# A two-layer mixer trunk on one core: the order of layer B's projection blocks, the pace of its convolutions, and the way its chunk-end decays are spread

## The chip, the cores and the metric

The kernel runs on one NeuronCore of one Trainium2 chip. The metric is the device time of one execution in microseconds (us). Before the change three runs gave 1652.05, 1648.64 and 1646.65 us; the median is 1648.64 us.

## The reference

A trunk of two layers over an input of 1024 tokens by 1024 features, float32. Each layer normalises, mixes, and adds to the stream; layer A is a chunked spatial gating unit, layer B a Mamba-2 state-space mixer. The change lies in the front part of layer B, which reads, cut down:

```python
proj = h @ w_in                                   # 1024 x 1024 by 1024 x 6176
z, xbc, dt_raw = proj[:2048], proj[2048:6144], proj[6144:]     # columns
xbc = silu(causal_depthwise_conv(xbc, conv_w, conv_b))         # 4 taps along the tokens
x, Bm, Cm = split(xbc)                                         # 8 groups of 256, 128, 128 columns
dt = softplus(dt_raw + dt_bias)                                # 32 heads
dA_cs = cumsum(dt * A, within each chunk of 128 tokens)
chunk_decay = exp(dA_cs[:, :, -1])                             # 8 chunks x 32 heads
# ... states, carried from chunk to chunk with chunk_decay; y; y * silu(z); norm; @ w_out
```

## The kernel before, in words

Matmuls are in float32 by three products of split operands: each operand is a high part (a cast, written on ACT, L111) and a low part (the rest, written on DVE, L112), and `mm3` (L134 to L136) issues high x high, low x high, high x low. A 128x512 output tile over 512 rows of depth is thus 12 matmuls; that is called a unit here.

Layer B's projection of z (four blocks `zb[0]` to `zb[3]`; `zb[3]` is narrow, 128 columns wide where the others have 256) and of half the groups of x, B and C (four blocks, `x` and `bc` for two pairs of groups) runs as blocks of Strassen's kind: seven products each, in the order 1, 2, 6, 7, 5, 4, 3, of two units each, or of one unit in the narrow block. ACT copies products 1, 6 and 7 to SBUF (`u`, L292); products 2, 5, 4 and 3 complete the quadrants C11, C22, C21 and C12. `into_b` runs `zb[0]` and the first product of `zb[1]`; `blocks` (L1400) runs the rest, in the order of its list `bs`. The weights of a block are loaded during the block before it (SP loads `wr`; POOL issues accumulating loads for sums and differences).

What is done with a quadrant:

- In a z block, an add on DVE (L960, except for C21, which is read from the accumulator), then SiLU on ACT (L965) and a store to DRAM, `z_d`, that ACT's queue issues (L966). SiLU and store are put off: a function goes into the list `late`.
- In an x or bc block, an add on DVE into `u` (L1304), a copy of three columns (`halo`, L1308), and one or two entries in the list `todo`: each is a convolution of a 128x512 tile. A convolution is an identity with scale and bias on ACT (L1271, into `xc`), three taps on DVE (L1265, and with a halo three small ones, L1268), SiLU on ACT (L1296) and a store from ACT's queue (L1297). SiLU and store go into `late`. A block leaves eight convolutions.

The order of the instructions is written out by hand here (`manual_schedule`): each engine has its instructions in the order in which the Python code issues them, and runs them strictly in that order. Ahead of each unit, `between` (L1412) runs the put-off work of `late`, and on odd turns, once the decays are through, also starts a convolution. Behind the last block convolutions are issued until three are left (`LEFT`), then the first split of plain weights (`next(pj)`) and a new set of PSUM pools, `new_psum` (L1455); the first matmuls of the plain projection write `ab`, in PSUM that the blocks' accumulators `acc` had. The rest of the convolutions is started by `scans`. During the last block, whose successor is none, three pieces of preparation for that projection are issued: the loads of its first weights at product 6, a load of 1 MB (`f01`) at product 7, and its split (`hh` and `hl`, 128x2048) at product 4.

`decays` (L1195) is a generator; `next(small)` advances it by one step at each unit, from the first unit of `blocks` on. It turns the raw `dt` into `dt`, `cs` (the cumulative sums) and `dtw` (`ecs` = exp(cs), `dte`), 32 heads by 128 tokens in four blocks of partitions. It stores `cs` and `ecs` to DRAM (L1234, eight stores of 32 KB, issued on SP's queue, two in each of four steps), and in the same steps the last column of each chunk of `ecs` to `dec_d` (L1237, eight stores of 32 single values each). Then PE transposes `dt`, `dte` and `cs` into PSUM tiles `tp` (L1246, two rotating buffers), one step each, and ACT copies each to `tk` (L1248) in the step behind. Last, SP loads `dec_d` broadcast over the partitions into `tk` (L1249).

Every DMA that SP's or ACT's queue issues signals one of eight completion counters, taken in turn; an issuing instruction waits until the DMA that used that counter before has landed.

Of the kernel before, what the change touches and what calls it, by code (L numbers as in the profile page):

```python
# [8 lines left out]
F32 = mybir.dt.float32  # L9
# [6 lines left out]
P = 128  # L16
# [7 lines left out]
NH = 32  # L24
# [5 lines left out]
def kernel(  # L30
# [21 lines left out]
    nc = tc.nc  # L52
    x = x[0]
    out = out[0]
# [8 lines left out]
    dr = ctx.enter_context(tc.tile_pool(name="dr", bufs=1, space=DRAM))  # L63

    def s8(shape, name, dt=F32):
        return sb.tile(shape, dt, name=name, tag="s8", bufs=16)

    def q4(shape, name):
        return sb.tile(shape, F32, name=name, tag="q4", bufs=6)

    def k2(shape, name, dt=F32):
        return sb.tile(shape, dt, name=name, tag="k2", bufs=4)
# [4 lines left out]
    def tiny(shape, name):  # L77
        return sb.tile(shape, F32, name=name, tag="tiny", bufs=8)
# [18 lines left out]
    def sm(name):  # L97
        return ps[0].tile([P, 512], F32, name=name, tag="sm", bufs=n_sm[0])
# [440 lines left out]
    tp = sm("tp")  # L539
# [12 lines left out]
    for gp in range(G // 2):  # L552
# [4 lines left out]
        if gp == 1:  # L557
# [9 lines left out]
            for h in range(2):  # L567
                tp = sm("tp")
# [5 lines left out]
                tp = sm("tp")  # L574
# [370 lines left out]
    late = []  # L945

    def finish():

        while late:
            late.pop(0)()  # L950
# [59 lines left out]
    zb = [z_block(b) for b in range(4)]  # L1010
# [184 lines left out]
    def decays():  # L1195

        dtw = q4([P, 4, 256], "dtw")
        cs = q4([P, 256], "cs")
        e_, s_, s2, p_ = (dtw[:, i, :] for i in range(4))
        V.scalar_tensor_tensor(e_, dtr, -1.0, dtr, ALU.mult, ALU.min)  # L1200
        nc.scalar.activation(e_, e_, AF.Exp)
        yield
        V.tensor_scalar(s_, e_, 2.0, None, ALU.add)
        V.reciprocal(s_, s_)
        V.tensor_tensor(s_, s_, e_, ALU.mult)
        V.tensor_tensor(s2, s_, s_, ALU.mult)
        V.tensor_scalar(p_, s2, 1.0 / 17, None, ALU.mult)
        for k in range(7, 0, -1):
            if k == 4:
                yield  # L1210
            V.scalar_tensor_tensor(p_, p_, 1.0 / (2 * k + 1), s2, ALU.add, ALU.mult)
        yield
        V.scalar_tensor_tensor(p_, p_, 1.0, s_, ALU.add, ALU.mult)
        V.tensor_scalar(s2, dtr, 0.0, None, ALU.max)
        dt = dtr
        V.scalar_tensor_tensor(dt, p_, 2.0, s2, ALU.mult, ALU.add)
        dA = dtw[:, 0, :]
        V.tensor_scalar(dA, dt, nA, None, ALU.mult)
        for j in range(2):
            V.tensor_tensor_scan(cs[:, j * P:(j + 1) * P], ones, dA[:, j * P:(j + 1) * P], 0.0, ALU.mult, ALU.add)  # L1220
        yield
        ecs = dtw[:, 1, :]
        nc.scalar.activation(ecs, cs, AF.Exp)
        dte = dtw[:, 2, :]
        for j in range(2):
            V.tensor_scalar(dte[:, j * P:(j + 1) * P], cs[:, j * P:(j + 1) * P], cs[:, j * P + P - 1:j * P + P], -1.0,
                            ALU.subtract, ALU.mult)
        yield
        nc.scalar.activation(dte, dte, AF.Exp)
        dec_d = dr.tile([8, NH], F32, name="dec_d")  # L1230
        for q in range(4):
            rs_ = slice(q * 32, (q + 1) * 32)
            for sc, src in ((cs_d, cs), (ecs_d, ecs)):
                nc.sync.dma_start(out=sc[2 * q:2 * q + 2].rearrange("c h l -> h c l"),  # L1234
                                  in_=src[rs_, :].rearrange("h (c l) -> h c l", c=2))
            for j in range(2):
                nc.sync.dma_start(out=dec_d[2 * q + j].rearrange("(h o) -> h o", o=1),  # L1237
                                  in_=ecs[rs_, j * P + P - 1:j * P + P])
            yield
        tk = s8([P, 2048], "tk")  # L1240
        tok = tk[:, 0:768].rearrange("p (v c r) -> p v c r", v=3, c=2)
        decb = tk[:, 768:1024]
        for i, src in enumerate((dt, dte, cs)):
            tp = sm("tp")
            for j in range(2):
                nc.tensor.transpose(out=tp[:, j * P:(j + 1) * P], in_=src[:, j * P:(j + 1) * P], identity=ident)  # L1246
            yield
            nc.scalar.copy(out=tok[:, i], in_=tp[:, 0:256].rearrange("p (c r) -> p c r", c=2))  # L1248
        nc.sync.dma_start(out=decb, in_=dec_d.rearrange("c h -> (c h)").partition_broadcast(P))  # L1249
        tok_of.update(tok=tok, decb=decb)  # L1250

    xbc_d, todo = {}, []

    def convolve():

        finish()
        if todo:
            late.append(todo.pop(0)())
# [15 lines left out]
    def xbc_block(kind, gs):  # L1274

        held, halos = {}, {}

        def cols(j):
            if kind == "x":
                return [(DI + gs[j] * 256, 256)]  # L1280
            return [(2 * DI + j * 1024 + g * P, P) for g in gs]

        def W(kh, j):
            return [b_w_in[kh * 512:(kh + 1) * 512, c:c + n] for c, n in cols(j)]

        def out(th, i, j, src, halo=None):
            if kind == "x":
                g, m, c = gs[j], i, cols(j)[0][0] + i * P
            else:
                g, m, c = gs[i], 2 + j, cols(j)[i][0]  # L1290
            dst = k2([P, 512], "xc")
            for op in conv_ops(dst, src, (c - DI) // P, halo):
                op()

            def rest():
                nc.scalar.activation(dst, dst, AF.Silu)  # L1296
                nc.scalar.dma_start(out=xbc_d[g][:, th, m, :], in_=dst)  # L1297

            return rest

        def done(name, i, a, u):
            th, j = 2 - int(name[1]), int(name[2]) - 1
            if u is not None:
                nc.vector.tensor_tensor(out=u, in0=a, in1=u, op=ALU.add)  # L1304
                a = u
            if th == 0:
                halo = halos[i, j] = tiny([P, 8], "halo")[:, 0:3]
                nc.vector.tensor_copy(out=halo, in_=a[:, 509:512])  # L1308
                todo.append(lambda: out(0, i, j, a))
                if (i, j) in held:  # L1310
                    todo.append(lambda: out(1, i, j, held[i, j], halo))
            elif (i, j) in halos:
                todo.append(lambda: out(1, i, j, a, halos[i, j]))
            else:
                held[i, j] = a

        return Block(H2, W, False, done, None)

    def rest_a21():
        raw = s8([P, 4, 512], "f01")  # L1320
        nc.sync.dma_start(out=raw, in_=f01_d)
        yield
        H2.update(new_H(("A21",)))
        split(*H2["A21"], raw)
# [75 lines left out]
    def blocks():  # L1400


        ORDER = (1, 2, 6, 7, 5, 4, 3)
        for g in SPILT:
            xbc_d[g] = dr.tile([P, 2, 4, 512], F32, name=f"xbc_d{g}")
        pairs = SPILT[:2], SPILT[2:]
        bs = [zb[1], xbc_block("x", pairs[0]), zb[2], xbc_block("bc", pairs[0]), zb[3], xbc_block("x", pairs[1]),
              xbc_block("bc", pairs[1])]
        seq = [(k, n) for k in range(len(bs)) for n in ORDER]
        small, turn, a21 = decays(), [0], rest_a21()  # L1410

        def between():  # L1412
            turn[0] += 1
            if next(small, 0) == 0 and turn[0] % 2:
                convolve()
            else:
                finish()

        for at, (k, n) in enumerate(seq[1:], 1):
            b, nxt = bs[k], bs[k + 1] if k + 1 < len(bs) else None  # L1420
            if at + 1 < len(seq):
                k2_, n2 = seq[at + 1]
                if n2 not in bs[k2_].Y:
                    bs[k2_].prep(n2)
            if n == 2:
                b.fourth()
            if nxt is not None:
                if n == 1 or at == 1:
                    nxt.load(0, 1)
                if n == 6:  # L1430
                    nxt.load(0, 0)
                elif n == 7:
                    nxt.sums_a()
                elif n == 5:
                    nxt.load(1, 0)
                    nxt.sums_b()
                elif n == 4:
                    nxt.load(1, 1)
            elif n == 6:
                next(pj)  # L1440
            elif n == 7:
                next(a21)
            elif n == 4:
                next(a21, None)
            for i in range(b.units):
                between()
                b.mm(n, i)
        while len(todo) > LEFT:
            convolve()

# [473 lines left out]
```

## Time and profile before

| what | value |
|---|---|
| median of three runs | 1648.64 us |
| the profiled execution: device time | 1643.76 us |
| the profiled execution: span of the trace | 1642.0 us |
| granted TensorE clock, mean | 0.965 |
| PE busy | 1511.4 us (92% of the span) |
| DVE busy | 1056.3 us (64%) |
| ACT busy | 775.9 us (47%) |
| POOL busy | 459.1 us (28%) |

The profile is one execution, recorded instruction by instruction. PE is the matmul engine, DVE VectorE, ACT ScalarE, POOL GpSimd, SP SyncE; `ACTq` and `SPq` are instructions with which ACT or SP issue DMAs. `L136` is line 136 of the kernel; `out<-in` names the tiles. An entry in square brackets is the idle time of the engine just before the instruction, and what ended it. The layer-B blocks discussed here take the time from about 793 to 1064 us of the span.

### The profile page before, as it was taken

What the parts mean: (1) busy time and instruction counts of PE and PEld (TensorE: products, weight loads), DVE (VectorE), ACT (ScalarE), POOL (GpSimd) and SP (SyncE); (2) the same over time, 40 slices, a digit from 0 to 9 for tenths busy, and PEclk for the clock granted to TensorE, in tenths of its full rate; (3) what the DMA queues carried; (4) which work ended last, traced back from release to release, by engine and by line L of the source; (5) the groups of instructions that cost most, each with busy time, mean ns of one, the idle gap of its engine ahead of it and who ended that gap; (6) DMA issues with size and microseconds to landing.
All of it is one profiled execution on the core that took longest, in us unless ns stands there. A gap on an engine that the chain in (4) does not pass through costs nothing.

```text
span 1642.0 us, 21287 instructions
## 1 busy us (share of the span) xinstructions
PE 1511.4 (92%) x7832; PEld 1242.2 (76%) x7832; DVE 1056.3 (64%) x1684; ACT 775.9 (47%) x1245; POOL 459.1 (28%) x466
## 2 busy tenths in 40 slices
PE   5799999999999999888979999969999999969988
PEld 5799988888888788766867777757777767747766
DVE  6966566666666545678525456756766767658746
ACT  4523233333333345545644455546666576543544
POOL 3601100000000141244301222116776756321231
PEclk7999999999999999988989999979999999979989
DMA  5154323333336999821577779745666675795992
GB/s 169 51 181 141 105 82 108 107 108 107 108 108 219 288 245 232 185 84 52 124 135 157 157 147 193 207 139 154 167 175 180 169 192 122 236 233 174 234 236 106
DMA packets 187784, 259.31 MB, mean 158 GB/s; under 512 B 16688, under 2 KB 117920, under 8 KB 184480
## 3 DMA queue, kind: packets, MB, share of 16 engines
q1 hardware_dynamic: 134672, 166.43, 33.9%
q0 software_dynamic: 39808, 70.53, 22.1%
q10 hardware_dynamic: 13200, 20.98, 3.6%
q8 instruction: 62, 1.02, 0.3%
q14 instruction: 42, 0.34, 0.1%
HBM read 183.65 MB, written 51.18 MB: 143 GB/s over the span
## 4 chain that ended last, share of the span: by engine, by line
PE 63%; DMA 12%; DVE 9%; ACT 8%; issue 5%; POOL 1%; ACTq 1%; SPq 1%; POOLq 0%; DVEq 0%
PE acc L136 12%; PE acc L134 11%; PE acc L135 11%; DMA wl<-cs_d 4%; PE ab L134 3%; PE ab L136 3%; PE ab L135 3%; PE ao L135 2%; PE ao L136 2%; PE ao L134 2%; PE yy L1557 2%; DVE xc L1265 2%; PE yy L1561 2%; PE mx L635 2%; DMA z_d<-zt 2%
## 5 line engine op out<-in xcount | busy, mean ns | idle before, releaser
L134 PE MATMUL acc<-hh,wh 128*128 128x512 f32 x868 | 344.3, 397 | 10.5 <-ACT wh L111 6.3
L136 PE MATMUL acc<-hh,wl 128*128 128x512 f32 x868 | 342.3, 394 | 6.0 <-DVE wl L112 6.0
L135 PE MATMUL acc<-hl,wh 128*128 128x512 f32 x868 | 340.8, 393 | 0.0
L112 DVE TENSOR_TENSOR wl<-wr,wh 128x1024 fp32r<-128x1024 f32 (+1 forms) x99 | 121.0, 1223 | 149.3 <-ACT wh L111 149.3
L134 PEld LDWEIGHTS acc<-hh,wh 128*128 128x128 f32 x868 | 165.1, 190 | 49.1 <-ACT wh L111 8.8
L136 PEld LDWEIGHTS acc<-hh,wl 128*128 128x128 f32 x868 | 164.8, 190 | 45.2 <-DVE wl L112 10.8
L135 PEld LDWEIGHTS acc<-hl,wh 128*128 128x128 f32 x868 | 164.8, 190 | 33.6
L111 ACT CAST wh<-wr 128x1024 fp32r<-128x1024 f32 (+1 forms) x113 | 116.4, 1030 | 109.3 <-PE acc L135 58.8
L292 ACT COPY u<-acc 128x512 f32<-128x512 f32 x117 | 67.9, 585 | 195.9 <-PE acc L136 191.4
L136 PE MATMUL acc<-wh,hl 128*128 128x256 f32 x448 | 130.4, 291 | 13.3 <-DVE hl L395 13.3
L134 PE MATMUL acc<-wh,hh 128*128 128x256 f32 x448 | 131.2, 293 | 4.1 <-DVE vt L331 2.5
L134 PE MATMUL ab<-hh,wh 128*128 128x512 f32 x256 | 116.8, 456 | 17.9 <-DVE xc L1265 17.9
L135 PE MATMUL acc<-wl,hh 128*128 128x256 f32 x448 | 129.7, 290 | 1.3 <-DVE wl L405 1.3
L1531 ACT ACTIVATE wl<-wl,tk 128x128 f32<-128x128 f32 x256 | 82.2, 392 | 80.3 <-DMA wl<-cs_d 80.0
L136 PE MATMUL ab<-hh,wl 128*128 128x512 f32 x256 | 101.7, 397 | 0.0
L135 PE MATMUL ab<-hl,wh 128*128 128x512 f32 x256 | 101.2, 395 | 0.0
L136 PEld LDWEIGHTS acc<-wh,hl 128*128 128x128 f32 x448 | 88.9, 199 | 14.4 <-DVE hl L395 14.4
L134 PE MATMUL bo<-wh,xh 128*128 128x512 f32 x192 | 80.5, 419 | 17.7 <-ACT xh L111 11.4
L112 DVE TENSOR_TENSOR xl<-ya,xh 128x1024 fp32r<-128x1024 f32 x40 | 49.0, 1224 | 68.7 <-ACT xh L111 68.7
L134 PEld LDWEIGHTS acc<-wh,hh 128*128 128x128 f32 x448 | 89.0, 199 | 5.2 <-issue 2.9
L135 PEld LDWEIGHTS acc<-wl,hh 128*128 128x128 f32 x448 | 89.0, 199 | 1.7 <-DVE wl L405 1.5
L111 ACT CAST xh<-ya 128x1024 fp32r<-128x1024 f32 x40 | 42.1, 1053 | 96.8 <-PE ao L135 43.1
(321 smaller groups left out, 3328.9 us busy)
## 6 DMA issues: line engine op xcount, KB each, us to landing
wr<-in_a_w_in_dram SPq DMA_DIRECT2D x48, 512.0 KB, 5.0
wl<-cs_d SPq DMA_DIRECT2D x64, 256.0 KB, 7.3
wr<-in_b_w_in_dram SPq DMA_DIRECT2D x30, 512.0 KB, 3.9
ya<-ya POOLq DMA_DIRECT2D x28, 512.0 KB, 15.1
wb<-in_a_w_out_dram SPq DMA_DIRECT2D x10, 1024.0 KB, 7.8
wb<-in_b_w_out_dram SPq DMA_DIRECT2D x10, 1024.0 KB, 13.5
wr<-in_b_w_in_dram SPq DMA_DIRECT2D x36, 256.0 KB, 8.2
v<-v_d SPq DMA_DIRECT2D x8, 1024.0 KB, 5.0
```

Source lines behind the costliest of these rows:

```text
L111: nc.scalar.copy(out=hi, in_=src)
L112: return (eng or nc.vector).tensor_tensor(out=lo, in0=src, in1=hi.bitcast(F32), op=ALU.subtract)
L134: nc.tensor.matmul(out=o, lhsT=l[0], rhs=r[0], start=start, stop=False, **kw)
L135: nc.tensor.matmul(out=o, lhsT=l[0], rhs=r[1], start=False, stop=False, **kw)
L136: nc.tensor.matmul(out=o, lhsT=l[1], rhs=r[0], start=False, stop=stop, **kw)
L292: nc.scalar.copy(out=self.u[n][:, i], in_=a)
L635: nc.tensor.matmul(out=mx[:, q * P:(q + 1) * P], lhsT=v[:, th * 4 + q, m * P:(m + 1) * P], rhs=mw[:, 0, :], start=True, stop=True)
L1265: nc.vector.scalar_tensor_tensor(dst[:, s:], src[:, :n - s], convw(3 - s, ch), dst[:, s:], ALU.mult, ALU.add)
L1531: nc.scalar.activation(wl[:, j, :], wl[:, j, :], AF.Relu, scale=-1.0, bias=tokc(2, c, self.g)[:, j:j + 1])
L1557: nc.tensor.matmul(out=yy[f * 64:(f + 1) * 64, pt * P:(pt + 1) * P], lhsT=w[:, j * 64:(j + 1) * 64], rhs=wl[:, j, :], start=True, stop=True)
L1561: nc.tensor.matmul(out=yy[:, 256 + pt * P:384 + pt * P], lhsT=self.state[c - 1][:, pt * P:(pt + 1) * P], rhs=self.x(3, c), start=True, sto ...
```

## The change

Four things, all inside `decays` and `blocks`:

1. In the list `bs` the narrow block `zb[3]` goes from the fifth place to the last; the second pair's x and bc blocks each move up by one.
2. `between` is replaced by `unit`. It sets the put-off work aside, starts a convolution if the decays are through and either the turn is odd or more than three are waiting, issues the unit's matmuls with the copies or adds behind them, and only then the put-off work.
3. `dec_d`, its eight stores and its broadcast load go. Instead ACT copies the last column of each chunk of `ecs`, broadcast to 128 columns, into the free quarter of `dtw` (`last`, two copies), PE transposes `last` like the three others, and ACT copies the result to `decb`.
4. `decays` has one step more behind the exponential of `dte`, and one more for the fourth transpose.

```diff
@@ decays
         nc.scalar.activation(dte, dte, AF.Exp)
-        dec_d = dr.tile([8, NH], F32, name="dec_d")
+        yield
         for q in range(4):
...
-            for j in range(2):
-                nc.sync.dma_start(out=dec_d[2 * q + j].rearrange("(h o) -> h o", o=1),
-                                  in_=ecs[rs_, j * P + P - 1:j * P + P])
             yield
...
-        for i, src in enumerate((dt, dte, cs)):
+        last = dtw[:, 3, :]
+        for j in range(2):
+            nc.scalar.copy(out=last[:, j * P:(j + 1) * P],
+                           in_=ecs[:, j * P + P - 1:j * P + P].broadcast_to([P, P]))
+        for i, src in enumerate((dt, dte, cs, last)):
...
-            nc.scalar.copy(out=tok[:, i], in_=tp[:, 0:256].rearrange("p (c r) -> p c r", c=2))
-        nc.sync.dma_start(out=decb, in_=dec_d.rearrange("c h -> (c h)").partition_broadcast(P))
+            if i < 3:
+                nc.scalar.copy(out=tok[:, i], in_=tp[:, 0:256].rearrange("p (c r) -> p c r", c=2))
+            else:
+                nc.scalar.copy(out=decb.rearrange("p (q j h) -> p j q h", q=4, j=2),
+                               in_=tp[:, 0:256].rearrange("p (j q h) -> p j q h", j=2, q=4))
@@ blocks
-        bs = [zb[1], xbc_block("x", pairs[0]), zb[2], xbc_block("bc", pairs[0]), zb[3], xbc_block("x", pairs[1]),
-              xbc_block("bc", pairs[1])]
+        bs = [zb[1], xbc_block("x", pairs[0]), zb[2], xbc_block("bc", pairs[0]), xbc_block("x", pairs[1]),
+              xbc_block("bc", pairs[1]), zb[3]]
...
-        def between():
+        def unit(b, n, i):
             turn[0] += 1
-            if next(small, 0) == 0 and turn[0] % 2:
-                convolve()
-            else:
-                finish()
+            off = late[:]
+            late.clear()
+            if next(small, 0) == 0 and todo and (turn[0] % 2 or len(todo) > 3):
+                late.append(todo.pop(0)())
+            b.mm(n, i)
+            for f in off:
+                f()
...
             for i in range(b.units):
-                between()
-                b.mm(n, i)
+                unit(b, n, i)
```

On SP, where the decays are stored (`cs`, `ecs` in `dtw`; `wr` is a load of weights), the kernel before has:

```order
L1234 DMA cs_d<-cs 32x2x128
L1234 DMA ecs_d<-dtw 32x2x128
L1237 DMA dec_d<-dtw 32x1 x2
L120 DMA wr<-in_b_w_in_dram 128x4x256
L1234 DMA cs_d<-cs 32x2x128
L1234 DMA ecs_d<-dtw 32x2x128
L1237 DMA dec_d<-dtw 32x1 x2
```

and the changed one, from the same place on:

```order
L1234 DMA cs_d<-cs 32x2x128
L1234 DMA ecs_d<-dtw 32x2x128
L1234 DMA cs_d<-cs 32x2x128
L1234 DMA ecs_d<-dtw 32x2x128
L120 DMA wr<-in_b_w_in_dram 128x4x256
L1234 DMA cs_d<-cs 32x2x128
L1234 DMA ecs_d<-dtw 32x2x128
```

The single-value stores are gone from between the pairs, and one load of weights that stood behind the first pairs now stands ahead of them.

On ACT, at the end of the blocks (the cast `wh` is for the plain projection, `xc` are convolutions, `zt` the z tiles, `acc` the blocks' accumulators), the kernel before has:

```order
L111 CAST wh_8214<-wr_8138 128x1024
L1296 ACTIVATE xc_8091<-xc_8091 128x512
L1297 DMA xbc_d5_6216<-xc_8091 128x512
L1271 ACTIVATE xc_8111<-acc_7820,par_867 128x512
L1296 ACTIVATE xc_8111<-xc_8111 128x512
L1297 DMA xbc_d3_6215<-xc_8111 128x512
L1271 ACTIVATE xc_8118<-u_7834,par_867 128x512
L1296 ACTIVATE xc_8118<-xc_8118 128x512
L1297 DMA xbc_d3_6215<-xc_8118 128x512
L1271 ACTIVATE xc_8128<-acc_7821,par_867 128x512
```

and the changed one, up to the first convolution of the plain projection (`x_8237<-ab_8188`):

```order
L111 CAST wh_8238<-wr_8162 128x1024
L966 DMA z_d6_5296<-zt_8106 128x512
L1275 ACTIVATE xc_8133<-u_7781,par_867 128x512
L965 ACTIVATE zt_8128<-acc_7980 128x512
L1300 ACTIVATE xc_8133<-xc_8133 128x512
L966 DMA z_d6_5296<-zt_8128 128x512
L1301 DMA xbc_d5_6216<-xc_8133 128x512
L965 ACTIVATE zt_8153<-zt_8153 128x512
L966 DMA z_d6_5296<-zt_8153 128x512
L1275 ACTIVATE x_8237<-ab_8188,par_867 128x1024
```

Before, convolutions follow each other there, two of them reading accumulators (`acc_7820`, `acc_7821`); now one convolution stands there, which reads `u`, and the SiLUs of the narrow block's last tiles, one of which reads an accumulator (`acc_7980`).

On ACT, during product 6 of `zb[2]` (`t12` is a weight sum to be cast for a later product), the kernel before has:

```order
L1271 ACTIVATE xc_6857<-acc_6507,par_867 128x512
L292 COPY u_6874<-acc_6769 128x512
L1296 ACTIVATE xc_6857<-xc_6857 128x512
L1297 DMA xbc_d0_6213<-xc_6857 128x512
L292 COPY u_6874<-acc_6770 128x512
L111 CAST wh_6891<-t12_6606 128x1024
```

and the changed one:

```order
L1275 ACTIVATE xc_6868<-u_6583,par_867 128x512
L292 COPY u_6888<-acc_6773 128x512
L965 ACTIVATE zt_6855<-zt_6855 128x512
L966 DMA z_d4_5294<-zt_6855 128x512
L292 COPY u_6888<-acc_6774 128x512
L1300 ACTIVATE xc_6868<-xc_6868 128x512
L1301 DMA xbc_d1_6214<-xc_6868 128x512
L111 CAST wh_6907<-t12_6602 128x1024
```

The convolution's SiLU and store stood ahead of the unit's second copy and now stand behind it; the cast stands behind both, as before.

## The prediction

> **What bounds the kernel now.** I read the page first (PE is busy 92% of the span), then, for the stretch that the change touches, PE's waits between 780 and 1120 us:
>
> ```profile
> PE ab L134 <- DVE xc L1265: 17.9, 1, 17.9
> PE tp L1246 <- ACT tk L1248: 8.2, 1, 8.2
> PE acc L134 <- ACT wh L111: 4.3, 4, 1.8
> PE acc L136 <- DVE wl L112: 2.8, 7, 0.5
> PE acc L134 <- ACT u L292: 2.7, 5, 0.8
> PE acc L134 <- ACT xc L1296: 1.4, 1, 1.4
> ```
>
> The columns are the total, the number of waits and the longest. PE bounds the stretch; two waits, 26.1 us together, stand out, and the blocks' other waits sum to 11.2 us. So the question is what these two hang on. The windows (us, then busy PE, PEld, DVE, ACT, POOL, granted clock, DMA share, GB/s) show each as a hole in PE, and the blocks between as nearly full:
>
> ```profile
> 823.60:831.80 8.20, 0.02 (x1) 0.00 (x0) 0.28 (x1) 1.95 (x4) 0.00 (x0) 0.64 1.44 159
> 832.00:1063.90 231.90, 221.01 (x938) 176.80 (x937) 132.24 (x206) 122.65 (x166) 46.32 (x36) 0.98 0.77 164
> 1063.90:1081.70 17.80, 0.03 (x1) 0.00 (x0) 11.77 (x16) 5.38 (x8) 2.75 (x1) 0.62 0.29 100
> ```
>
> In the first hole nobody computes and the DMA share is high: a transfer is waited for. In the second DVE is busy for 11.8 of 17.8 us: work is waited for.
>
> The first hole, on ACT's timeline and on the chain of waits:
>
> ```profile
> 830.08 0.33 ACTq L966 DMA_DIRECT2D z_d<-zt  x1
> 830.44 1.04 ACT L111 CAST wh<-wr 128x1024 fp32r<-128x1024 f32 x1 [6.21 <-DMA z_d<-zt]
> 831.39 0.37 ACT L1248 COPY tk<-tp 128x256 f32<-128x256 f32 x1
> ```
>
> ```profile
> 814.06 15.94 DMA z_d<-zt
> ```
>
> ACT's queue stands at the issue of a `z_d` store until 830.08, since an earlier `z_d` store with the same completion counter, issued at 814.06, lands only after 15.94 us. Behind it in ACT's order stand a cast and the copy of the transpose; PE's third transpose needs that copy for its buffer. So PE waits for a slow store. Three kinds of transfer between 806 and 841 us (size, median time to landing), then `z_d` between 885 and 930 us:
>
> ```profile
> cs_d<-cs SPq DMA_DIRECT2D x4, 32.0 KB, 9.6
> ecs_d<-dtw SPq DMA_DIRECT2D x4, 32.0 KB, 7.0
> dec_d<-dtw SPq DMA_DIRECT2D x8, 0.1 KB, 15.0
> ```
>
> ```profile
> z_d<-zt ACTq DMA_DIRECT2D x8, 256.0 KB, 2.9
> ```
>
> The same store lands in 2.9 us later on and takes 15.94 us here. The slowest beside it, by far the slowest for their size, are the `dec_d` stores: 128 bytes in 15.0 us. On SP they hold the queue, too:
>
> ```profile
> 823.04 5.19 SPq L1237 DMA_DIRECT2D dec_d<-dtw  x2
> ```
>
> **Part by part: the decays.** The change takes away the eight `dec_d` stores, and their broadcast load. With them the reason that I see for the slow landing goes, the `z_d` store is back near 2.9 us, and ACT does not stand. PE's rows there:
>
> ```profile
> 831.81 0.69 PE L1246 MATMUL tp<-ident,cs 128*128 128x128 f32 x2 [8.19 <-ACT tk L1248]
> 832.15 0.78 PE L134 MATMUL acc<-hh,wh 128*128 128x512 f32 x1
> ...
> 835.71 0.56 PE L136 MATMUL acc<-hh,wl 128*128 128x512 f32 x1
> ```
>
> ```profile
> 1063.32 0.39 PE L135 MATMUL acc<-hl,wh 128*128 128x512 f32 x1
> 1063.55 0.39 PE L136 MATMUL acc<-hh,wl 128*128 128x512 f32 x1
> 1081.78 0.77 PE L134 MATMUL ab<-hh,wh 128*128 128x512 f32 x1 [17.85 <-DVE xc L1265]
> ```
>
> Removed are 8.19 us of waiting, and the slow matmuls behind it: from 832.15 to 835.71 eight matmuls take 3.56 us, at the usual 0.23 each (1063.32 to 1063.55) 1.84, so 1.7 us are lost there. Added are the two transposes of `last` (0.69 us by the row of two) and three ACT copies (0.37 us each by the copy's row, a gap in ACT's use). The copies lie beside matmuls. The transposes lie on PE: +0.35 to +0.7, and I take 0.5, between half of the row and the whole, since the row stands among slow matmuls. The extra steps of `decays` shift the transposes by a unit, and the turn from which convolutions may start from the 12th to the 14th. The first x block has its first convolution ready at about the 21st, so this costs nothing; without that slack it would be one convolution put off, 3.3 us of ACT and DVE. **Sum: -8.2 - 1.7 + 0.5 = -9.4 us.** Its bounds: -10 if the transposes hide, and -2.2 if the stall stays (first rival).
>
> Here the Trainium skill says two things, both in "DMA: Bandwidth & Descriptors". Its section "Specifications" says that transfers in pieces below 512 bytes make the DMA engine read, modify and write; the trace agrees in the one number it has, 15.0 us for a store of 4-byte pieces. Its section "Rules for kernel authors" says that transfers under 64 KB are mostly overhead; that speaks against a full gain, since the eight 32 KB stores stay. By the first rule the term would be the -9.4 us above; by the second alone it would be the first rival's -2.2.
>
> **Part by part: the end of the blocks.** Now the last matmul of the blocks is followed on ACT by a cast, then by convolutions; two of them read accumulators whose space `ab` takes, and DVE still has taps to do:
>
> ```profile
> 1063.99 1.03 ACT L111 CAST wh<-wr 128x1024 fp32r<-128x1024 f32 x1
> ...
> 1074.07 0.81 ACT L1271 ACTIVATE xc<-u,par 128x512 f32<-128x512 f32 x1 [0.40 <-ACT xc L1296]
> ...
> 1078.13 0.33 ACTq L1297 DMA_DIRECT2D xbc_d<-xc  x1
> 1078.51 0.78 ACT L1271 ACTIVATE xc<-acc,par 128x512 f32<-128x512 f32 x1 [0.40 <-ACT xc L1296]
> ```
>
> ```profile
> 1054.39 1.22 DVE L112 TENSOR_TENSOR wl<-wr,wh 128x1024 fp32r<-128x1024 f32 x1
> 1055.53 2.29 DVE L112 TENSOR_TENSOR hl<-f,hh 128x2048 fp32r<-128x2048 f32 x1
> ...
> 1077.16 0.21 DVE L1268 SCALAR_TENSOR_TENSOR xc<-halo,par,xc 128x3 f32<-128x3 f32 x1
> 1079.32 2.32 DVE L1265 SCALAR_TENSOR_TENSOR xc<-acc,par,xc 128x511 f32<-128x511 f32 x3 [1.94 <-ACT xc L1271]
> ```
>
> PE starts at 1081.78 (row above), 0.14 us behind the end of the last taps of an accumulator (1079.32 + 2.32): this is what it waits for, 17.85 us. With a z block last, only one convolution stands behind the cast in the order of ACT, and the accumulators are released by a SiLU and by the add of C12. That add stands on DVE behind the convolution's taps. The path from the last matmul: the cast 1.03; the issue of a store, 0.38 (1078.13 to 1078.51); identity and taps with halo, 3.30 (1074.07 to 1077.16 + 0.21); the add, 0.69:
>
> ```profile
> L960 DVE TENSOR_TENSOR zt<-acc,u 128x512 f32<-128x512 f32 x2 | 1.4, 687 | 0.9 <-PE acc L136 0.9
> ```
>
> Together 5.4 us. **The term is 5.4 - 17.85 = -12.4 us.** The slow matmuls at a start after a gap stay. Below, 4.0 us if the cast is through early; above, some 9 us if DVE comes late into the end. For that I add up DVE in the narrow block, which lasts 7 units x 12 x 0.2275 = 19.1 us on PE: adds, and low parts of narrow weights of the same 128x512 shape, at 0.69, some ten of them, 6.9; two `wl` at 1.22, 2.4; `hl` 2.29; four convolutions at 2.3 to 2.5, 9.6; 21 us in all with the last convolution, which already stands in the gap. So DVE is just through.
>
> **Part by part: the middle.** Convolutions on every unit while more than three wait, and put-off work behind the copies. Total work of DVE stays; it moves forward, into 231.9 us of which DVE uses 132.2 now. Some nine convolutions more at 2.4 us make 154 of 232, so on average there is room. Locally there isn't: a product of two units lasts 5.46 us on PE; two convolutions (4.8), one `wl` (1.22) and two adds (1.4) ask 7.4 us of DVE. A lag of 2 us a product for one or two products is hidden by the preparation, which is issued a product ahead (5.46 less the 2.3 us of cast and `wl` leaves 3.2 us); beyond that it costs. For the change speak the 2.7 and 1.4 us for `u` and for a SiLU: a SiLU and a store ahead of a copy no longer hold PE's buffer. I take -2 for these, +1 for the lag, **-1 us**, with bounds -4 (all of both waits) and +5 (a lag of 2 to 3 us laid bare at two changes of block).
>
> Moving the narrow block also moves its loads and its accumulating loads behind the others'. One of these was late already:
>
> ```profile
> 980.29 15.45 DMA t<-in_b_w_in_dram
> ```
>
> It is on the chain now and stood in front of the narrow block's products. I cost it at nothing: the neighbouring block is two products of lead away; the cover gone, it is 0 to 6 us (second rival).
>
> **Sum:** -9.4 - 12.4 - 1 = -22.8 us. The profiled execution took 1643.76 us (span 1642.0), which would become 1621.0. The median of the three runs, 1648.64, lies 4.9 us above the profiled one; on it the forecast is **1625.8 us**.
>
> **The rivals.** *First: the slow landing stays.* What holds the queues may be the eight 32 KB stores, which land in 7 to 9.6 us themselves, or POOL's accumulating loads, whose queue (packets, MB, share of 16 engines) between 823.6 and 831.8 holds most of the DMA engines' time:
>
> ```profile
> q0 software_dynamic: 732, 0.72, 87.0%
> ```
>
> Then ACT still stands until about 830, and PE gains only the one unit (2.73 us) by which the transposes come later, less 0.5: -2.2 instead of -9.4, so 1633.0. For it: 87%; against it: the accumulating loads hold the engines later, too, with `z_d` at 2.9 us. Chance 0.23.
>
> *Second: the end waits for a load.* The cast ahead of everything on ACT needs a weight load that is issued in the short last block, and the 1 MB load for `hl` comes there too. If one lands 6 to 7 us late (the 15.45 us row shows that a load can be late by as much), the gap stays near 12: +6.6, 1632.4. Chance 0.08; with the first together 1639.6, chance 0.05.
>
> *Third: DVE becomes the bound.* If convolutions come on both units of a product, about half of the 32 stand in front of a `wl` for which PE waits, and the lead is used up, each costs up to its 2.4 us on PE: 16 x 2.4 = 38 us, less 22.8: +16, 1664. It decides from the point where PE's waits in the blocks (11.2 us now) exceed 34 us. Against it: the average of 154 in 232 us. Chance 0.07.
>
> *Fourth: nothing comes of it.* The holes stay, since behind the convolutions another release of `ab`'s space is as late (the f01 split, a SiLU in ACT's order behind a waiting issue), and the first rival holds: -2, 1646. Chance 0.07.
>
> **How the numbers follow.** The forecast has 0.50, the rivals 0.23, 0.08, 0.05, 0.07 and 0.07. The range goes from 1616 (all bounds below: -10, -13.9 and -4 give 1621, and the runs of before reach from 2 us below to 3.4 above their median; some of the other 7 us of waits may go with the two) to 1641 (forecast with the middle at +5 and the end at 9, or the first two rivals together). It leaves out the two last rivals, 0.14. A difference of 0.3%, 5 us, is about what a measurement of this kernel can tell from none. Faster by more: 0.50 + 0.23 + 0.08 + 0.05 = 0.86; same 0.07; slower 0.07.
>
> **What would show it.** Right: no wait of PE at the transposes above 1 us, `z_d` landing in 3 to 4 us between 806 and 841, and one wait of 4 to 7 us at the first `ab`, ended by the add L960. First rival: a wait of about 5.5 us at the third or fourth transpose behind a `z_d` issue. Second: the wait at `ab` above 9 us, with the cast of `wh` ended by a DMA. Third: waits of PE for `wl` over 20 us in total. The forecast is wrong as a whole if the blocks from the first unit to the first `ab` are not at least 15 us shorter.

## The result, and the profile after

The changed kernel takes 1624.22 us (median of four runs, 1620.58 to 1628.66) where before takes 1649.2. The ratio is 0.985, interval 0.982 to 0.988: 25 us less, with 1625.8 us forecast. The profiled execution has a span of 1618.9 us, 23.1 less than before.

PE's waits in the changed kernel between 780 and 1110 us (total, times, longest). Line numbers have moved: the taps are L1269 now, a convolution's identity L1275, its SiLU L1300.

```profile
PE ab L134 <- ACT xc L1300: 8.7, 1, 8.7
PE acc L134 <- ACT wh L111: 5.6, 3, 2.2
PE acc L136 <- DVE wl L112: 1.6, 3, 0.5
PE acc L134 <- ACT u L292: 1.3, 3, 0.7
PE acc L134 <- DVE zt L960: 0.4, 1, 0.4
```

The wait at a transpose is gone, the one at the first `ab` has halved, the blocks' other waits have gone from 11.2 to 8.9 us. The first `ab` matmul, which ends the part that was changed, starts here:

```profile
1058.49 0.77 PE L134 MATMUL ab<-hh,wh 128*128 128x512 f32 x1 [8.68 <-ACT xc L1300]
```

Before it started at 1081.78. So 23.3 us of the difference lie ahead of it, which is the whole difference of the two spans; behind it nothing is won.

For comparing profiled executions a stretch between two instructions is sharper than the time of the whole. It is taken here from the first step of `decays`, at the first unit of `blocks`, to the first `ab`. The first step before, in the changed kernel, and in e10 below:

```profile
795.79 0.42 DVE L1200 SCALAR_TENSOR_TENSOR dtw<-dtr 128x256 f32<-128x256 f32 x1
795.65 0.42 DVE L1200 SCALAR_TENSOR_TENSOR dtw<-dtr 128x256 f32<-128x256 f32 x1
793.94 0.42 DVE L1200 SCALAR_TENSOR_TENSOR dtw<-dtr 128x256 f32<-128x256 f32 x1
```

What lies ahead of the stretch and behind it is the same work in all kernels here, yet it varies: the first step comes between 793.94 us (e10) and 798.83 (e1), and the time behind the first `ab` goes from 559.9 us (e2) to 569.4 (e6). The stretch is 286.0 us before and 262.8 in the changed kernel, 23.2 less.

The 23.3 us to the first `ab` are 9.2 at the end of the blocks and 14.1 ahead of their last matmul. Two windows, one of each kernel, from 778 us to that last matmul (PE, PEld, DVE, ACT, POOL, granted clock, DMA share, GB/s), first before, then after:

```profile
778.00:1063.93 285.93, 266.63 (x1139) 212.96 (x1137) 157.33 (x246) 152.18 (x205) 59.55 (x43) 0.98 0.76 158
```

```profile
778.00:1049.80 271.80, 262.82 (x1140) 211.91 (x1138) 166.25 (x271) 157.15 (x215) 59.56 (x43) 0.99 0.74 163
```

PE's idle time fell from 19.3 to 9.0 us, 10.3 less, and its busy time by 3.8, for as many matmuls: the granted clock went from 0.98 to 0.99. DVE does 9 us more in a window that is 14 us shorter.

The transfers at the first hole's place, 806 to 841 us:

```profile
z_d<-zt ACTq DMA_DIRECT2D x6, 256.0 KB, 5.2
```

That is a median of the two whose landing the profile tells, 3.5 and 6.9 us. One took 15.94 us before; the prediction had 3 to 4. The packets of SP's queue show the relief with all of them counted (packets, MB, share of 16 engines between 806 and 841 us, before and after):

```profile
q1 hardware_dynamic: 2739, 1.96, 43.8%
q1 hardware_dynamic: 2499, 2.10, 20.9%
```

Without the single-value stores slightly more bytes take less than half of the time. The end of the blocks, on DVE, then on POOL and on the chain:

```profile
1048.72 2.29 DVE L112 TENSOR_TENSOR hl<-f,hh 128x2048 fp32r<-128x2048 f32 x1 [1.52 <-ACT hh L111]
1050.93 2.35 DVE L112 TENSOR_TENSOR wl<-wr,wh 128x1024 fp32r<-128x1024 f32 x2
1053.32 2.72 DVE L1269 SCALAR_TENSOR_TENSOR xc<-u,par,xc 128x511 f32<-128x511 f32 x1
...
1057.53 0.21 DVE L1272 SCALAR_TENSOR_TENSOR xc<-halo,par,xc 128x3 f32<-128x3 f32 x1
1057.66 0.68 DVE L960 TENSOR_TENSOR zt<-acc,u 128x512 f32<-128x512 f32 x1
```

```profile
1052.65 2.83 POOL L112 TENSOR_TENSOR wl<-wr,wh 128x1024 fp32r<-128x1024 f32 x1 [17.30 <-ACT wh L111]
```

```profile
1038.50 7.29 DMA f<-f_d
```

The order of work is the one forecast: one convolution, then the add that frees the last accumulator, then PE. (The profile names the convolution's SiLU as the releaser, since it ends at the same moment, 1058.47; in the program PE waits for the add, which ends 0.15 us before PE starts, and for a SiLU that had ended at 1057.62.) But the first tap takes 2.72 us where its like takes 0.75, and it starts late, since ACT is behind: the split of the 1 MB load `f` waited for its landing, and the last cast starts 1.7 us behind the last matmul, which ended at 1049.81.

```profile
1046.78 1.91 ACT L111 CAST hh<-f 128x2048 fp32r<-128x2048 f32 x1 [2.77 <-DMA f<-f_d]
1048.59 1.04 ACT L111 CAST wh<-wr 128x1024 fp32r<-128x1024 f32 x1
...
1051.53 1.03 ACT L111 CAST wh<-wr 128x1024 fp32r<-128x1024 f32 x1
```

### The profile page after: what moved, and what is told of

Its sections match the earlier page's. It is cut to its first block, busy times and chain, and to the rows that moved or that the text cites. A ratio compares the mean times of both kernels' runs of the same rounds, so it can differ in the third digit from the quotient of the medians.

```text
span 1618.9 us, 21275 instructions
## 1 busy us (share of the span) xinstructions
PE 1507.8 (93%) x7834; PEld 1241.1 (77%) x7834; DVE 1056.2 (65%) x1684; ACT 775.8 (48%) x1248; POOL 458.4 (28%) x466
## 4 chain that ended last, share of the span: by engine, by line
PE 57%; issue 15%; DMA 10%; DVE 8%; ACT 7%; POOL 1%; SPq 1%; ACTq 0%; POOLq 0%; DVEq 0%
PE acc L136 10%; PE acc L134 9%; PE acc L135 9%; DMA wl<-cs_d 4%; PE ab L134 3%; PE ab L136 3%; PE ab L135 3%; PE ao L135 3%; PE ao L134 3%; PE ao L136 3%; PE yy L1564 2%; PE yy L1568 2%; DVE wl L112 2%; DVE xc L1269 2%; DMA wb<-in_b_w_out_dram 1%
## 5 line engine op out<-in xcount | busy, mean ns | idle before, releaser
L136 PE MATMUL acc<-wh,hl 128*128 128x256 f32 x448 | 130.2, 291 | 12.4 <-DVE hl L395 12.4
L136 PEld LDWEIGHTS acc<-wh,hl 128*128 128x128 f32 x448 | 88.9, 198 | 13.5 <-DVE hl L395 13.5
L134 PE MATMUL bo<-wh,xh 128*128 128x512 f32 x192 | 80.5, 419 | 16.1 <-ACT xh L111 11.9
```

What stands on the lines that cost most here:

```text
L134: nc.tensor.matmul(out=o, lhsT=l[0], rhs=r[0], start=start, stop=False, **kw)
L136: nc.tensor.matmul(out=o, lhsT=l[1], rhs=r[0], start=False, stop=stop, **kw)
```

## The experiments

Ratios are to the kernel before, run on the same chip, with 95% intervals. The stretch is that of the section above, and the wait at the first `ab` is a part of it; both are in us, from one profiled execution each. The changed kernel, profiled twice, differs by 1.6 us in the stretch.

| kernel | ratio | stretch | wait at the first `ab` |
|---|---|---|---|
| before | 1 | 286.0 | 17.9 |
| changed | 0.985 | 262.8 | 8.7 |
| changed again (e5) | 0.9862 | 261.3 | 7.8 |
| decays alone (e1) | 0.9944 | 274.7 | 17.6 |
| order alone (e2) | 1.0 | 286.4 | 13.0 |
| pace alone (e3) | 0.9947 | 279.9 | 10.5 |
| changed, single-value stores back (e4) | 0.9953 | 277.4 | 7.8 |
| changed, old order (e6) | 0.9865 | 263.8 | 10.5 |
| changed, more 32 KB stores (e7) | 0.9877 | 265.6 | 8.6 |
| changed, no late convolutions (e8) | 0.9826 | 256.1 | 2.3 |
| changed, odd turns only (e9) | 0.9913 | 271.9 | 12.0 |
| changed, put-off work ahead (e10) | 0.9869 | 266.5 | 6.9 |
| changed, low part on DVE (e11) | 0.9839 | 262.4 | 8.2 |

### The decays alone (e1)

Before with the `decays` of the change, nothing else:

```diff
-        dec_d = dr.tile([8, NH], F32, name="dec_d")
+        yield
...
-                nc.sync.dma_start(out=dec_d[2 * q + j]...
...
-        for i, src in enumerate((dt, dte, cs)):
+        for i, src in enumerate((dt, dte, cs, last)):
```

> The kernel before with the changed decays alone (no single-value stores, fourth transpose, the extra steps); old block order, old pace. My theory (the 4-byte stores make everything on the queues land late): the wait of 8.2 us at the third transpose goes, z_d between 806 and 841 us lands in 3 to 5 us, and the time falls by 9.4 us, to about 1640 where before has 1649; the wait of 17.9 us at the first ab stays. Rival (the eight 32 KB stores or POOL's loads keep the queues slow): a wait of about 5.5 us at a transpose stays and the time falls by 2 us.

Ratio 0.9944 (0.9924 to 0.9964): 9.2 us less, with 9.4 expected. The wait at the transposes is gone, the other stays:

```profile
PE ab L134 <- DVE xc L1269: 17.6, 1, 17.6
PE acc L134 <- ACT wh L111: 4.5, 4, 1.8
```

### The single-value stores put back (e4), and 32 KB stores in their place (e7)

```diff
 # e4: the changed kernel, in the step that stores cs and ecs
+            for j in range(2):
+                nc.sync.dma_start(out=dec_d[2 * q + j].rearrange("(h o) -> h o", o=1),
+                                  in_=ecs[rs_, j * P + P - 1:j * P + P])
```

```diff
 # e7: the changed kernel, at the same place
+            for j in range(2):
+                nc.sync.dma_start(out=dup_d[j, 2 * q:2 * q + 2].rearrange("c h l -> h c l"),
+                                  in_=(cs, ecs)[j][rs_, :].rearrange("h (c l) -> h c l", c=2))
```

> The changed kernel with the eight stores of single values put back at their old places, into a DRAM tensor that nothing reads; everything else as changed. My theory (the 4-byte pieces are what is slow): z_d stores issued between 806 and 841 us take 10 us or more to land again, ACT stands at one of their issues, PE waits 5 us or more at a transpose, and the time rises by 6 to 10 us over the changed kernel, to some 1630 to 1634. Rival (the stall went because the steps moved by a unit, or because of the broadcast load): within 2 us of the changed kernel, 1624.

> The changed kernel with eight more stores of 32 KB (copies of cs and ecs into DRAM that nothing reads) at the places where before had its single-value stores: as many instructions on the same queue, 256 times the bytes, in pieces of 512 bytes. Theory (the 4-byte pieces are the cause): z_d between 806 and 841 us still lands in about 6 us, no wait above 2 us at a transpose, the time within 3 us of the changed kernel. Rival (the number of small stores on the queue is the cause): a wait of 5 us or more at a transpose, the time up by 6 to 17 us.

With the single-value stores: 0.9953 (0.9938 to 0.9968), 15 to 17 us above the changed kernel, more than expected. With eight 32 KB stores: 0.9877 (0.9855 to 0.9899), within its interval of the changed kernel (0.9862 on the same chip). Eight instructions on the same queue in both. In the stretch the single-value stores cost 14.6 to 16.2 us, the 256 times larger ones 2.8 to 4.4, too little for the times to show. ACT in the first of the two:

```profile
829.77 0.33 ACTq L966 DMA_DIRECT2D z_d<-zt  x1
830.14 1.04 ACT L111 CAST wh<-wr 128x1024 fp32r<-128x1024 f32 x1 [9.60 <-DMA z_d<-zt]
...
840.54 0.33 ACTq L966 DMA_DIRECT2D z_d<-zt  x1
840.90 0.37 ACT L1254 COPY tk<-tp 128x256 f32<-128x256 f32 x1 [8.83 <-DMA z_d<-zt]
```

and its waits of PE:

```profile
PE tp L1251 <- ACT tk L1254: 13.1, 1, 13.1
PE ab L134 <- ACT xc L1304: 7.8, 1, 7.8
```

It is the same mechanism as in before (ACT stands at the issue of a `z_d` store, and PE waits for the copy behind it), with a wait of 13.1 us instead of 8.2. In the kernel with 32 KB stores the transfers between 806 and 841 us, and the waits at the transposes, are as follows (each landing time rests on one store of its row, the one that the profile tells):

```profile
z_d<-zt ACTq DMA_DIRECT2D x6, 256.0 KB, 3.9
dup_d<-cs SPq DMA_DIRECT2D x4, 32.0 KB, 6.5
dup_d<-dtw SPq DMA_DIRECT2D x4, 32.0 KB, 3.6
```

```profile
PE tp L1251 <- ACT tk L1254: 0.8, 2, 0.5
```

So it is the single-value stores with their 4-byte pieces, not the number of stores: the first rival falls, and with it POOL's loads, which stand in all these kernels. Their destination was not tested apart from the size of the pieces: the eight stores write neighbouring rows of 128 bytes in one tensor of 1 KB. The steps and the broadcast load are out as causes too, since e4 has the new steps and no such load.

### The order alone (e2), and the whole without the order (e6)

```diff
 # e2: before with this alone; e6: the changed kernel with this undone
-        bs = [..., zb[3], xbc_block("x", pairs[1]), xbc_block("bc", pairs[1])]
+        bs = [..., xbc_block("x", pairs[1]), xbc_block("bc", pairs[1]), zb[3]]
```

> The kernel before with the narrow block last, and nothing else. In its order of instructions one convolution from u and one from an accumulator stand between the last low part of weights and the first ab. Theory 1 (order and pace each take most of the end's wait, and overlap): the wait at the first ab is 5.4 us plus one more convolution of 4.4 us, some 10 to 13 us, and the time falls by 5 to 8 us. Theory 2 (the pace does it, the order is idle): the wait stays above 16 us and the time within 2 us of before. The 8.2 us at the transpose stay in both.

> The changed kernel with the old order of the blocks (narrow block fifth): pace and decays changed, order not. Alone, the order brought nothing, decays 9 us and pace 9 us, 18 together, where the whole change has brought 25. Theory 1 (the order saves only behind the new pace, since only then is the list of convolutions down to two when the narrow block ends): this kernel gains 18 us (ratio 0.989), with a wait of 10 to 11 us at the first ab. Theory 2 (the missing 7 us are the spread of the first measurement): this kernel is within 3 us of the changed one.

The order alone: 1.0 (0.9986 to 1.0015). The whole change without it: 0.9865 (0.9841 to 0.9889), and 0.9862 (0.9843 to 0.9881) with it, in a second measurement of the changed kernel (e5):

> The changed kernel itself, unchanged, on the chip of the next three runs, so that they can be compared with it closely. Ratio to before 0.985 as first measured; waits of PE as in the first profile: 8 to 9 us at the first ab, none above 1 us at a transpose.

The order brings nothing that the times show, alone or with the rest. In e2 theory 1 was right on the wait at the end and wrong on the time, and in e6 theory 1 fell: the missing 7 us are not the order's. PE's waits with the order alone show where its gain went:

```profile
PE ab L134 <- DVE xc L1265: 13.0, 1, 13.0
PE tp L1246 <- ACT tk L1248: 9.2, 1, 9.2
PE acc L134 <- ACT wh L111: 6.4, 5, 1.8
PE acc L134 <- ACT u L292: 4.4, 6, 1.1
PE acc L136 <- DVE wl L112: 3.4, 8, 0.5
```

4.8 us off the end's wait, as expected; 1.0 more at the transpose and 3.0 more inside the blocks (14.2 against 11.2). So the narrow block costs inside the blocks what it saves behind them, and the stretch is as long as before (286.4 and 286.0 us). With the new pace and decays the old order (e6) has a wait of 10.5 us against 8.7 and 7.8 with the new one, and a stretch longer by 1.0 to 2.6 us: there the order may be worth that much, but the changed kernel's own two profiles differ by 1.6 us.

### The pace alone (e3), and its two halves (e9, e10)

```diff
 # e3: before with unit() for between(); e9: the changed kernel with
-            if next(small, 0) == 0 and todo and (turn[0] % 2 or len(todo) > 3):
+            if next(small, 0) == 0 and todo and turn[0] % 2:
 # e10: the changed kernel with
+            for f in off:
+                f()
             b.mm(n, i)
-            for f in off:
-                f()
```

> The kernel before with the new pace alone (a convolution on every unit while more than three wait, put-off work behind the copies); old block order, old decays. Theory 1 (overlap): the wait at the first ab falls to 8 to 10 us, since only one convolution from u and one from an accumulator are left behind the last block; the time falls by 8 to 10 us. Theory 2 (the order does it): the wait stays above 15 us, the time within 3 us. The third rival of the prediction (DVE becomes the bound) would show as waits of PE for wl above 20 us in the blocks, and a longer time.

> The changed kernel with convolutions on odd turns only, as before; the put-off work stays behind the copies, order and decays as changed. Theory (what shortens the end is that the list is down to two by then, which takes the extra convolutions): behind the last block one convolution from u and one from an accumulator are left on DVE, the wait at the first ab is 11 to 13 us where the changed kernel has 8, and the time is 3 to 5 us above the changed kernel (ratio to before 0.988 to 0.990). Rival (the place of the put-off work makes the gain of the pace): within 1.5 us of the changed kernel.

> The changed kernel with the put-off work ahead of a unit's matmuls and copies again; the extra convolutions, order and decays as changed. By the prediction's middle term PE's waits for u rise by about 2 us and a SiLU is waited for again; the time is 1 to 3 us above the changed kernel. Rival (the place of the put-off work is idle): within 1 us, and the waits for u stay at 1 to 1.5 us.

The pace alone: 0.9947 (0.993 to 0.9964), 8.7 us; the wait at the first `ab` is 10.5 us, just above the 8 to 10 that overlap had said. Odd turns only: 0.9913 (0.9896 to 0.9929), 8 us above the changed kernel, with

```profile
PE ab L134 <- DVE xc L1269: 12.0, 1, 12.0
PE acc L134 <- ACT wh L111: 7.6, 6, 2.1
```

as expected at the end; the time lost was 4 us more than expected, since the waits in the blocks rose as well (13.3 us, 8.5 in e5). With the put-off work ahead: 0.9869 (0.9848 to 0.989), which the intervals do not tell from the changed kernel. Its place does move waits:

```profile
PE ab L134 <- ACT xc L1300: 6.9, 1, 6.9
PE acc L134 <- ACT u L292: 6.2, 5, 2.4
PE acc L134 <- ACT wh L111: 3.2, 3, 1.8
```

The waits for `u` are 6.2 us against 1.1 in e5, those for `wh` 3.2 against 5.3, the end 6.9 against 7.8; all of PE's waits together are 17.9 us against 16.3. The stretch is 3.7 to 5.2 us longer than in the changed kernel's two profiles, since PE's busy time ahead of the last matmul is longer too (248.6 us for 1062 matmuls, 245.0 for 1063 in e5). In that profile more matmuls ran slowly behind gaps, which differs from one execution to another (last section). So whether the place of the put-off work is worth its 2 us stays open. The larger part of the pace's gain is the extra convolutions: without them 8 us in time and 9.0 to 10.6 us of the stretch are lost. They do not show as waits for `wl` (1.6 us in the changed kernel): the rival with DVE as the bound falls.

### What is left at the end (e8, e11)

```diff
 # e8: the changed kernel with
-            if next(small, 0) == 0 and todo and (
+            if next(small, 0) == 0 and todo and not (b is bs[-1] and n in (4, 3)) and (
 # e11: the changed kernel with
-                split(*W[i, kh], raw.pop((i, kh)), nc.gpsimd if i else V)
+                split(*W[i, kh], raw.pop((i, kh)), nc.gpsimd if i > 1 or (i and kh) else V)
```

> The changed kernel with no convolution started in products 4 and 3 of the last block, so that the add that frees the last accumulator stands on DVE right behind the weights' low part, not behind six taps. Theory (the 8.7 us at the first ab are the taps, one of them slowed to 2.7 us, and the add): the wait falls to 3 to 5 us, held then by the 1 MB load and its split, and the time falls by 4 to 5 us below the changed kernel. Rival (the load of 1 MB, which can be issued only after product 7 of the last block, or the SiLU that waits for a store to land, sets the wait anyway): the wait stays above 7 us and the time within 2 us.

> The changed kernel with one low part of weights (128x1024, the first of the second plain set) made on DVE and not on POOL. In the profiles so far the DVE instruction that runs beside that POOL instruction takes 2 us longer than its like (2.72 us for a tap of 0.75). Theory (POOL's work holds DVE's instruction): every tap of the last convolution takes 0.75 us, DVE has 1.2 us more to do, and the wait at the first ab falls by some 0.7 us. Rival (something else holds the tap, as the landing of data): a tap of over 2 us stays there, and the wait grows by 1.2 us.

Without the late convolutions: 1616.49 us, 0.9826 (0.98 to 0.9851), the fastest of all, some 6 us below the changed kernel on the same chip (the two intervals still touch; the stretch is 5.2 us shorter than in e5). The add follows the low part of the weights, and PE comes behind it:

```profile
1052.36 1.22 DVE L112 TENSOR_TENSOR wl<-wr,wh 128x1024 fp32r<-128x1024 f32 x1
1053.50 0.69 DVE L960 TENSOR_TENSOR zt<-acc,u 128x512 f32<-128x512 f32 x1
```

```profile
1054.55 0.49 PE L134 MATMUL ab<-hh,wh 128*128 128x512 f32 x1 [2.32 <-ACT zt L965]
1054.88 0.39 PE L135 MATMUL ab<-hl,wh 128*128 128x512 f32 x1
1055.11 0.40 PE L136 MATMUL ab<-hh,wl 128*128 128x512 f32 x1
```

The gap is 2.32 us instead of 8.68, lower than expected, and with so short a gap the matmuls behind it run at 0.23 us from the start: the slow restart is saved as well in this execution. What bounds the end now is the 1 MB load (7.39 us on the chain) with its cast and its low part. This is where the new order pays: with a z block last there is nothing behind the last matmul but SiLUs and one add, if the convolutions keep away. With a bc block last, the last accumulators still have to be convolved. No run has the old order without late convolutions, so that the order is needed for this gain is argued, not shown.

With the low part made on DVE: 0.9839 (0.9815 to 0.9863), no difference from the changed kernel in time. The tap is what it shows:

```profile
1054.63 0.75 DVE L1269 SCALAR_TENSOR_TENSOR xc<-u,par,xc 128x511 f32<-128x511 f32 x1
```

It takes 0.75 instead of 2.72 us with POOL idle there, and the wait falls by 0.5 us (8.68 to 8.19), DVE having 1.2 us more to do. POOL's work held the tap.

## Why the prediction was right, point by point

- **The bound and the two holes**: right. All that was won lies ahead of the first `ab`, none behind it.
- **The decays, -9.4 us**: right in mechanism and, alone, in size (9.2 us in time, 11.3 in the stretch). Beside the new pace they are worth more: 13.5 us by the ratios of e6 and e3, 16.1 by their stretches, and 15 to 17 us by e4. The same slow stores make PE wait 9.8 us at a transpose in e3 and 13.1 in e4, in place of 8.2. That the parts add up to the total was an assumption of the sum. Alone, decays, pace and order give 9.2, 8.7 and 0 us, together 18, and 23 to 25 came; in the stretch they give 11.3, 6.1 and -0.4, together 17.0, and 23.2 to 24.7 came. Of the 4.8 us by which 16.1 exceeds 11.3, 1.6 are the longer wait at the transpose (9.8 against 8.2) and 2.7 are waits for `wh`, which the decays shorten beside the new pace (6.9 us in e3, 4.2 in e6) and not alone (4.3 before, 4.5 in e1). Why they do was not taken apart. A small slip without weight in the sum: by the steps of `decays`, twelve before and fourteen now, convolutions may start from the 13th and the 15th unit, not the 12th and the 14th.
- **The end, -12.4 us**: the term was mis-sized, -9.2 measured. The gap was to be 5.4 us and is 8.7, outside the 4 to 7 us that were to be its sign. The step that failed is the path from the last matmul: the cast was to start at once, and started at 1051.53, 1.7 us behind the end of the last matmul at 1049.81, as ACT was behind; the profile puts that to the 1 MB load, which landed late and held the casts ahead (the second rival in small, below the 9 us that were its mark); an earlier load wasn't tried, since its buffer comes free only behind product 7 of the last block. And the taps were taken at 3.30 us from identity to end; the first was held by POOL for 2.0 us.
- **Why the end got better**: the prediction put it to the z block standing last. That is the smaller part of it. Alone the order takes 4.8 us off the wait and the pace 7.3; with the rest changed, the order takes 1.8 to 2.7 (e6) and the extra convolutions 3.3 to 4.2 (e9, where the wait is 12.0 us). What the order wins there, alone, it gives back ahead of the last matmul, and the change without the order is as fast as the times can tell. The extra convolutions, which the prediction had as a cost of the middle, are what shortened the list.
- **The middle, -1 us**: the waits fell by 2.3 us, and 2.1 us more of slow matmuls went than the 1.7 of the first hole (3.8 in all). The 2 us given to the place of the put-off work are neither shown nor refuted: without it PE's waits are 1.6 us longer and one profile's stretch 3.7 to 5.2, but the times do not differ. The lag of DVE, feared up to +5, is not seen.
- **The third and fourth rivals** are refuted by the waits for `wl` (1.6 us) and by the result.

So the end gave 3.2 us less than the sum had, and the part ahead of the last matmul, with 14.1 us against the 10.4 of the other two terms, 3.7 more. That the total came within 2 us of the forecast is partly luck: the two errors cancel.

On the DMA rules: the Trainium skill, "DMA: Bandwidth & Descriptors", section "Specifications", says that pieces below 512 bytes cost a read-modify-write. The runs fit that: beside stores of 4-byte pieces a `z_d` store took 15.94 us (before) and 13.22 (e4), beside 32 KB stores in 512-byte pieces 3.9 (e7). That a read-modify-write is what holds the others is not shown by them. The Trainium skill's rule on the same page that transfers under 64 KB are mostly overhead ("Rules for kernel authors") is no guide here: by it alone the decays would have won 2.2 us, where they won 9.2, and eight stores of 32 KB more cost at most 2.8 to 4.4 us of the stretch.

The landing times that this rests on are few: the 15.0 us of `dec_d` are one of eight stores, and in e4 the two that the profile tells took 6.9 and 13.7 us. The runs with and without the stores carry the argument.

## What to carry to other kernels

When a store of a few bytes shares completion counters with large ones, look at who stands at the next issue: its price is paid on another engine, and an extra transpose beside the matmuls is cheaper. At a change of stage, list what still has to run on each engine between the last matmul and the first one of the next stage, with the loads that can only be issued late; keep work that nobody waits for out of that list. Try the parts of a change alone and taken out of the whole: here the order did nothing alone, and the decays were worth 9 us alone and 13 to 17 beside the new pace.

## What the runs showed of the hardware

- POOL's TENSOR_TENSOR from SBUF held a DVE instruction with two SBUF inputs: a tap of 0.75 us took 2.72 and ended 0.56 us behind POOL's instruction of 2.83 us; it took 0.75 with that work taken off POOL. The Trainium skill's "SBUF — State Buffer", section "SBUF: two separate sides", calls the port pair that the two share an exclusive lock; the rows agree.
- 128 bytes in 4-byte pieces landed in 6.9 to 16.7 us, where the profile tells it. The slowest 256 KB store beside them took 13.2 to 17.0 us (before, e2, e3, e4); without them such stores took 2.4 to 7.4 (changed kernel, e1, e5, e6, e7).
- After a gap of 2.32 us PE came back at full pace (e8), after 8.7 us at half: matmuls 0.43 us apart. A gap of about 2 us can go either way: at the same place in the blocks, 2.18 us in the changed kernel were followed by matmuls 0.23 us apart, 2.17 us in e7 by matmuls 0.43 us apart.
